# Small transfers of a two-layer block moved between issuing queues: ScalarE's to SyncE's, one store from SyncE's to GpSimd's

## The chip, the cores and the metric

The kernel runs on one core of a Trainium2 chip. The metric is the device time of one execution in microseconds (us), the median of several runs. A profile of one execution shows what each engine did: PE (TensorE matmul) and PEld (its weight load), DVE (VectorE), ACT (ScalarE), POOL (GpSimd) and SP (SyncE). SP computes nothing; it only issues transfers. ACT and POOL both compute and issue. Each engine takes its instructions in one fixed order. "ACTq", "SPq" and "POOLq" in a row are the instructions of an engine's sequencer: transfers that it issues, waits, branches.

## The reference

Two layers of a transformer-like block on 512 latent tokens and 256 context tokens, 1024 wide. Cut to what matters:

```python
def trunk_layer(x, xc, c, c_ctx, last, ...):
    mod = silu(c) @ w_mod + b_mod                  # sh1, sc1, gt1, sh2, sc2, gt2
    proj = (x * (1 + sc1) + sh1) @ w_in            # and the same for the context
    yr = rwkv_mixer(...)                           # two directions, 4 heads of 64
    ys = s5_mixer(...)
    ya = attention_mixer(...)                      # window of 128 tokens, context, sink
    mix = concat([yr, ys, ya]) @ w_out
    x = layer_norm(ALPHA * x + gt1 * mix, ln1_g, ln1_b)
    h = x * (1 + sc2) + sh2
    y = hier_moe(h, ...)                           # 32 experts, 2 for each token
    x = layer_norm(ALPHA * x + gt2 * y, ln2_g, ln2_b)
```

The recurrent part of `rwkv_mixer` is, for each token and head, `s = s * w - (s kk) b + v k`, read out by `r`, forwards and backwards. The output is `x` of the 512 latent tokens.

## The kernel before

Each layer goes through the same stages, one after the other: the input projections with the S5 mixer (`input_side`); then RWKV, with attention, the modulation and parts of the output product laid between its steps (`rwkv`, `attention`, `mod_unit`, `mixing`); then the norms and the routing (`norm`, `Route`); then the 32 experts, whose weights are streamed from memory (`experts`); then `combine`.

RWKV works on tiles of 128 tokens, six of them in the first layer.

- `front(i)` (from L367) loads a tile of the convolved projections, computes decay, keys, values and gates, and stores them in DRAM tensors from which later steps load them in another layout: `rec` (keys `kh`, the gated keys `bt`, the values) at L461, and `atd` at L462.
- `back(i)` (from L465) loads the values back in chunks of 64 tokens (`vz`, L474), transposes with TensorE, copies from PSUM with ScalarE (`ar` L483, `bz` L495, `r` L517), forms the score matrices, and stores them: `rec` at L485 and L509, `sca` at L507, `atd` at L518.
- `inverse(b)` (from L524) loads 32x32 blocks of `sca` at L540, inverts them by substitution on VectorE and GpSimd at once, and stores the inverses at L557 to L562.
- `solve(i, d)` (from L564) loads for one tile and direction a block of scores (L571), `atd` (L573), and the inverses (L576, L578), and stores its results in `rec` at L609 and L610.
- `step(n, d)` (from L616) loads a chunk of `rec` (L625) and takes the recurrence one chunk further; `finish` (L687 on) normalizes.

Up to the change, the transfers of one such step are divided between the queues of SP and ACT: at L461 the values go out by SP, the keys by ACT; at L540 the blocks of one direction by SP, of the other by ACT; in `solve` the block of scores and one inverse by SP, `atd` and the other inverse by ACT.

`mod_unit` (L114 on) computes 128 columns of the modulation: it loads 512 KB of `w_mod` by SP (L118, two buffers), has TensorE multiply them (L127), and copies the result with ScalarE (`mres`, L129). For every 512 columns of the later four parts it loads the bias row `mrow` (L122, one buffer), adds the products to it (L141), and stores it (L143), so the next load of `mrow` waits for that store.

The units of attention, modulation and mixing that are laid between RWKV's steps are counted out by the table `FILL`; `fill('front')`, `fill('back')` and so on take so many of them. Within the stage the order on each queue is not that of the text: a planner lays out each engine's instructions when the program is built, so a transfer that goes to another queue may also be given another place.

`norm(i)` (L1621 on) ends in `affine` (L1658 on): ACT scales the tile, POOL multiplies and adds a row (L1661, L1662), and SP stores the result as `x1` (L1663), which `combine` loads after the experts. SP's queue also carries the experts' weights (L1824).

The transfers of the change in the text before:

```python
for src, r, c, q in ((kh[:, d], 0, 0, nc.scalar), (bt[:, d], 64, 0, nc.scalar), (VT[i], 0, 256, nc.sync)):
    q.dma_start(rec[z, :, r:r + 64, c:c + 256], src)        # L461
nc.scalar.dma_start(vv[0:64], rec[slot[i, 0], :, 0:64, 256:512]...)   # L474
nc.sync.dma_start(x1[r], t)                                  # L1663
```

Of the kernel before, what the change touches and what calls it, by code (L numbers as in the profile page):

```python
# [61 lines left out]
def row(ap):  # L62

    return ap.rearrange("(o n) -> o n", o=1)
# [49 lines left out]
def mod_unit(k, l, mp, c0, n, bufs=2):  # L114

    nc = k.nc
    wt = mp.tile([128, 8, n], F32, name='wmod', bufs=bufs)
    nc.sync.dma_start(wt, k.a['w_mod'][l].rearrange("(p k) n -> p k n", k=8)[:, :, c0:c0 + n])  # L118
    v, f = c0 // 1024, c0 % 512
    if v >= 2 and f == 0:  # L120
        k.mrow = mp.tile([2, 512], F32, name='mrow', bufs=1)
        nc.scalar.dma_start(k.mrow, row(k.a['b_mod'][l, c0:c0 + 512]).to_broadcast([2, 512]))  # L122
    b = k.bank()
    p = b[:, 0:n]
    for kk in range(8):
        g = kk % 4
        nc.tensor.matmul(p[32 * g:32 * g + 32, :], k.cc[:, kk, :], wt[:, kk, :], start=kk < 4, stop=kk >= 4, tile_position=(0, 32 * g))  # L127
    r = mp.tile([128, n], F32, name='mres', bufs=bufs)
    nc.scalar.copy(r, p)  # L129
    p2 = b[:, n:] if n < 512 else k.bank()  # L130
    if v < 2:
        cols, bc = k.cols[l]
        j0, m = c0 // 128, n // 128
        for j in range(m):
            nc.tensor.matmul(p2[:, 2 * j:2 * j + 2], r[:, 128 * j:128 * j + 128], k.sel, start=True, stop=True)
        nc.vector.scalar_tensor_tensor(cols[:, v, j0 % 8:j0 % 8 + m, :], p2[:, 0:2 * m].rearrange("p (j s) -> p j s", s=2), float(v),
                                       bc[:, j0:j0 + m, None].to_broadcast([128, m, 2]), op0=ALU.add, op1=ALU.add)
        return
    nc.tensor.matmul(p2[0:2, 0:n], k.sel, r, start=True, stop=True)
    o = k.mrow[:, f:f + n]  # L140
    nc.vector.scalar_tensor_tensor(o, p2[0:2, 0:n], 1.0 if v == 4 else 0.0, o, op0=ALU.add, op1=ALU.add)  # L141
    if f + n == 512:
        nc.scalar.dma_start(k.dram('modrow%d' % l, [2, 4, 1024])[:, v - 2, c0 % 1024 - f:c0 % 1024 + n], k.mrow)  # L143

# [178 lines left out]
def rwkv(k, l, st, cvd, Y, ys, streams, fill):  # L325


    nc, tc = k.nc, k.tc
# [7 lines left out]
    V, G, A = nc.vector, nc.gpsimd, nc.scalar  # L336

    rec = k.dram('rec%d' % l, [12, 2, 128, 1024])
    sca = k.dram('sca%d' % l, [12, 8, 128, 64])
    atd = k.dram('atd%d' % l, [12, 128, 2, 256])  # L340
# [6 lines left out]
    GM, VT, GL = {}, {}, {}  # L347
# [3 lines left out]
    inv_o = k.dram('inv_out', [96, 64, 64])  # L351
# [15 lines left out]
    def front(i):  # L367
# [89 lines left out]
        for d in range(2):  # L457
            z = slot[i, d]

            for src, r, c, q in ((kh[:, d], 0, 0, nc.scalar), (bt[:, d], 64, 0, nc.scalar), (VT[i], 0, 256, nc.sync)):  # L460
                q.dma_start(rec[z, :, r:r + 64, c:c + 256], src)  # L461
            nc.sync.dma_start(atd[z, :, 0], at[:, d, :])  # L462
        F[i] = at, rh, bt, kh

    def back(i):  # L465

        out = emit_ctx or i >= 2
        k.stream = GS
        at, rh, bt, kh = F.pop(i)
        n = 2 if out else 1  # L470
        j = len(done) % 2
        done.append(i)
        vv = vz[j]
        nc.scalar.dma_start(vv[0:64], rec[slot[i, 0], :, 0:64, 256:512].rearrange("c t x -> t c x"))  # L474
        for d in range(2):
            z = slot[i, d]

            ar = Fp.tile([128, 2, 2, 2, 64], F32, name='ar', bufs=2)
            p = k.bank()
            for s, src in ((0, at), (1, rh))[0:n]:  # L480
                for q in range(2):
                    tr(k, p[:, 256 * s + q * 128:256 * s + q * 128 + 128], src[:, d, q * 128:q * 128 + 128])
                A.copy(ar[:, s].rearrange("p c q t -> p q c t"), p[:, 256 * s:256 * s + 256].rearrange("p (q c t) -> p q c t", q=2, c=2))  # L483
            if out:
                nc.scalar.dma_start(rec[z, :, :, 640:768].rearrange("c p x -> p c x"), ar[:, 1].rearrange("p c q t -> p c (q t)"))  # L485

            bk = bz[(2 * j + d) % 2]
            p = k.bank()
            for s, src in ((0, bt), (1, kh)):
                for q in range(2):  # L490
                    tr(k, p[:, 256 * s + q * 128:256 * s + q * 128 + 128], src[:, d, q * 128:q * 128 + 128])
                pv = p[:, 256 * s:256 * s + 256].rearrange("p (q c t) -> p q c t", q=2, c=2)
                for hp in range(2):
                    r_ = slice(64 * hp, 64 * hp + 64)
                    A.copy(bk[r_, hp, :, :, 1 - s, :], pv[r_])  # L495

            sc = Fp.tile([128, 2, 2, 2, 2, 64], F32, name='sc', bufs=2)
            for hp in range(2):
                p = k.bank()
                pv = p.rearrange("p (c q s t) -> p c q s t", c=2, q=2, s=2)  # L500
                for q in range(2):
                    for cp in range(2):
                        nc.tensor.matmul(pv[:, cp, q, 0:n, :], bk[:, hp, q, cp].rearrange("p s t -> p (s t)"),  # L503
                                         ar[:, 0:n, cp, q, :], start=True, stop=True)
                for s in range(n):
                    V.tensor_tensor(sc[:, s, :, hp], pv[:, :, :, s, :], k.msk[d][:, None, s:s + 1, :].to_broadcast([128, 2, 2, 64]), op=ALU.mult)
            nc.sync.dma_start(sca[z].rearrange("a p t -> p a t"), sc[:, 0].rearrange("p c h q t -> p (c h q) t"))  # L507
            if out:
                nc.sync.dma_start(rec[z, :, :, 768:1024].rearrange("c p x -> p c x"), sc[:, 1].rearrange("p c h q t -> p c (h q t)"))  # L509

            p = k.bank()
            for h in range(4):
                q, hp = divmod(h, 2)
                for cp in range(2):
                    nc.tensor.matmul(p[64 * cp:64 * cp + 64, 64 * h:64 * h + 64], sc[:, 0, cp, hp, q, :], vv[:, cp, 64 * h:64 * h + 64], start=True, stop=True)
            r1 = Fp.tile([128, 256], F32, name='r1', bufs=2)
            A.copy(r1, p[:, 0:256])  # L517
            nc.scalar.dma_start(atd[z, :, 1], r1)  # L518

    def dblk(ap, s0, q):  # L520

        return bass.AP(tensor=ap.tensor, offset=ap.offset + s0 * 4096 + 2080 * q, ap=[[4096, 24], [64, 32], [1, 32]])

    def inverse(b):  # L524


        R = 4
# [8 lines left out]
        for q in range(2):  # L536
            for d, t, o in ((0, Bm, 24 * q), (1, tm, 64 + 24 * q)):
                src = bass.AP(tensor=sca.tensor, offset=sca.offset + (6 * b + 3 * d) * 65536 + (64 + 32 * q) * 64 + 32 * q,
                              ap=[[8192, 24], [64, 32], [1, 32]])
                (nc.scalar if d else nc.sync).dma_start(t[o:o + 24], src)  # L540
        V.tensor_copy(Bm[64:112], tm[64:112].rearrange("p i t -> p t i"))
        for x, r0, n in ((Xl, 0, R), (Xh, R, 32 - R)):
            G.memset(x, 0.0)
# [11 lines left out]
        for q in range(2):  # L555
            f, v = slice(24 * q, 24 * q + 24), slice(64 + 24 * q, 88 + 24 * q)
            nc.sync.dma_start(dblk(inv_o, s0, q)[:, 0:R], Xl[f])  # L557
            nc.sync.dma_start(dblk(inv_o, s0, q)[:, R:32], Xh[f])
            nc.scalar.dma_start(dblk(inv_o, s0 + 24, q), tm[v])
        nc.sync.dma_start(inv_t[s0:s0 + 24], tm[0:24])  # L560
        nc.scalar.dma_start(inv_t[s0 + 24:s0 + 48, 0:R], Xl[88:112])
        nc.scalar.dma_start(inv_t[s0 + 24:s0 + 48, R:32], Xh[88:112])  # L562

    def solve(i, d):  # L564

# [4 lines left out]
        ab = Q.tile([128, 8, 32], F32, name='ab', bufs=SB)  # L570
        nc.sync.dma_start(ab[u:u + 32], sca[z, :, u:u + 32, v:v + 32].rearrange("a p t -> p a t"))  # L571
        at = Q.tile([128, 2, 256], F32, name='atl', bufs=SB)
        nc.scalar.dma_start(at, atd[z])  # L573
        x = Q.tile([128, 4, 64], F32, name='x', bufs=SB)
        for cp in range(2):
            nc.sync.dma_start(x[64 * cp:64 * cp + 64], inv_o[s0 + 4 * cp:s0 + 4 * cp + 4].rearrange("h i t -> i h t"))  # L576
        t = Q.tile([128, 8, 32], F32, name='xt', bufs=SB)
        nc.scalar.dma_start(t[u:u + 32], inv_t[s0:s0 + 8].rearrange("h i t -> i h t"))  # L578

        p = k.bank()  # L580
        w = Q.tile([128, 4, 32], F32, name='xw', bufs=2)
# [18 lines left out]
        for cp in range(2):  # L600
# [5 lines left out]
                nc.tensor.matmul(p[64:128, 256 + 64 * h:320 + 64 * h], x[own[cp], hq, :], at[own[cp], 1, 64 * h:64 * h + 64], start=True, stop=True)  # L606
            A.activation(xa[:, cp], p[:, 0:128], AF.Copy, scale=-1.0)
            V.tensor_scalar(W[64:128, cp], p[64:128, 256:512], -1.0, None, op0=ALU.mult)
        nc.scalar.dma_start(rec[z, :, :, 512:640].rearrange("c p x -> p c x"), xa)  # L609
        nc.sync.dma_start(rec[z, :, 64:128, 256:512].rearrange("c t x -> t c x"), W[64:128])  # L610

    chain = (tuple(range(12)), (3, 2, 1, 0, 11, 10, 9, 8, 7, 6, 5, 4))
# [934 lines left out]
def mixing(k, l, sO, sR, before, yd, ys, x_src, x1, hd, NTOK):  # L1547
# [73 lines left out]
    def norm(i):  # L1621
# [36 lines left out]
        def affine():  # L1658
            V.tensor_scalar(sb[:, 1:2], mv[:, 0:1], sb[:, 0:1], -1.0, op0=ALU.mult, op1=ALU.mult)
            A.activation(t, t, AF.Identity, bias=sb[:, 1:2], scale=sb[:, 0:1])  # L1660
            G.tensor_tensor(t, t, lg, op=ALU.mult)  # L1661
            G.tensor_tensor(t, t, lb, op=ALU.add)  # L1662
            nc.sync.dma_start(x1[r], t)  # L1663
        return hT, affine

    groups = [g for g in ((0, 1), (3, 4), (2, 5)) if g[0] >= t0]
# [603 lines left out]
```

## Time and profile before

| | |
|---|---|
| time before, median of 3 runs | 2894.11 us (2893.8 to 2897.02) |
| the profiled execution's own time | 2882.98 us |
| its span, first to last instruction | 2881.2 us |
| granted TensorE clock, mean of the span | 0.871 of full speed |
| PE busy | 2219.2 us (77%) |
| PEld busy | 1487.5 us (52%) |
| DVE busy | 1185.8 us (41%) |
| POOL busy | 823.0 us (29%) |
| ACT busy | 523.3 us (18%) |

The profiled execution took 2882.98 us, of which 2881.2 us are its span. Busy time leaves out what a sequencer does, so the time in which ACT issues a transfer, or waits to be allowed to, is idle time of ACT in this table. A row on a wait names the engine and line that waited and, behind the arrow, what ended the wait; "issue" stands for time in which the profile shows nothing that was waited for.

### The profile page before, as it was taken

What the parts mean: (1) busy time and instruction counts of PE and PEld (TensorE: products, weight loads), DVE (VectorE), ACT (ScalarE), POOL (GpSimd) and SP (SyncE); (2) the same over time, 40 slices, a digit from 0 to 9 for tenths busy, and PEclk for the clock granted to TensorE, in tenths of its full rate; (3) what the DMA queues carried; (4) which work ended last, traced back from release to release, by engine and by line L of the source; (5) the groups of instructions that cost most, each with busy time, mean ns of one, the idle gap of its engine ahead of it and who ended that gap; (6) DMA issues with size and microseconds to landing.
All of it is one profiled execution on the core that took longest, in us unless ns stands there. A gap on an engine that the chain in (4) does not pass through costs nothing. (4 is left out here: it accounts for less than half of the span.)

```text
span 2881.2 us, 43454 instructions
## 1 busy us (share of the span) xinstructions
PE 2219.2 (77%) x16189; PEld 1487.5 (52%) x16189; DVE 1185.8 (41%) x2830; ACT 523.3 (18%) x1264; POOL 823.0 (29%) x1131
## 2 busy tenths in 40 slices
PE   5898677789874978989955787677898488788882
PEld 4786445567432544555525675455555254454441
DVE  7872554665556100000016873456645711111113
ACT  3222233223001100001015222233110100000001
POOL 2651322431544011101016652333324510111002
PEclk8999788789986999999987898579699699999996
DMA  8334466665627899989974324446784589998995
GB/s 241 93 94 116 141 179 185 175 189 163 220 93 265 351 418 371 391 329 379 388 279 121 83 56 142 117 128 161 212 244 140 230 355 418 416 379 331 384 419 201
DMA packets 404797, 691.34 MB, mean 240 GB/s; under 512 B 134755, under 2 KB 310627, under 8 KB 388097
## 3 DMA queue, kind: packets, MB, share of 16 engines
q1 hardware_dynamic: 311808, 600.10, 58.1%
q10 hardware_dynamic: 78880, 64.32, 7.5%
q0 software_dynamic: 13792, 22.61, 2.1%
q8 instruction: 211, 3.46, 0.5%
q14 instruction: 106, 0.86, 0.1%
HBM read 607.98 MB, written 95.44 MB: 244 GB/s over the span
## 5 line engine op out<-in xcount | busy, mean ns | idle before, releaser
L1762 PE MATMUL b_m<-w,xT 128*64 128x256 f32 x4928 | 593.7, 396 | 128.8 <-DMA w<-in_expert_w_gate_dram 80.2
L1762 PEld LDWEIGHTS b_m<-w,xT 128*64 128x64 f32 x4928 | 391.9, 142 | 333.3 <-issue 148.0
L243 PE MATMUL b_m<-xT,win 128*128 128x256 f32 (+1 forms) x1416 | 275.8, 355 | 7.0 <-POOL xT L167 3.5
L243 PEld LDWEIGHTS b_m<-xT,win 128*128 128x128 f32 x1416 | 232.8, 202 | 41.0 <-POOL xT L167 4.4
L1786 PE MATMUL b_m<-w,aT 128*64 128x512 f32 x1024 | 231.0, 592 | 1.1 <-issue 0.6
L1775 DVE COPY aT<-b_m 128x256 f32<-128x256 f32 x64 | 27.2, 425 | 474.4 <-PE b_m L59 474.4
L1792 POOL DMA_INDIRECT yb<-y,dx x64 | 63.9, 998 | 419.7 <-DVEq L1907 245.2
L1786 PEld LDWEIGHTS b_m<-w,aT 128*64 128x64 f32 x1024 | 76.2, 137 | 117.3 <-issue 108.3
L1764 ACT ACTIVATE act<-b_m 128x256 f32<-128x256 f32 x64 | 24.6, 384 | 566.8 <-PE b_m L1762 566.8
L1765 DVE TENSOR_TENSOR act<-act,b_m 128x256 f32<-128x256 f32 x64 | 27.0, 422 | 233.5 <-PE b_m L1762 233.5
L877 PE MATMUL b_a<-kz,qb 128*128 128x128 f32 (+2 forms) x416 | 111.9, 415 | 8.2 <-ACT pr L898 6.1
L1582 PE MATMUL b_a<-wo,yt 128*128 128x512 f32 x240 | 112.4, 618 | 0.0
L1792 POOL DMA_INDIRECT yb<-yo,dx x13 | 12.9, 994 | 291.7 <-ACTq L1907 166.2
L127 PE MATMUL b_a<-wmod,cc 128*32 128x128 f32 x1280 | 64.2, 315 | 40.0 <-DMA wmod<-in_w_mod_dram 28.0
L877 PEld LDWEIGHTS b_a<-kz,qb 128*128 128x128 f32 x416 | 78.2, 237 | 32.2 <-issue 13.0
L59 PE MATMUL b_a<-idf,pr 128*128 128x128 f32 x320 | 58.4, 304 | 34.3 <-DVE pt L921 11.5
L503 PE MATMUL b_g<-ar,bz 128*128 128x128 f32 (+1 forms) x384 | 66.2, 337 | 11.7 <-ACT bz L495 11.6
L1855 POOL DMA_INDIRECT xg<-hd,ix x32 | 33.0, 1031 | 146.8 <-PE b_m L59 105.2
L503 PEld LDWEIGHTS b_g<-ar,bz 128*128 128x128 f32 x384 | 61.8, 248 | 22.3 <-ACT bz L495 18.0
L1582 PEld LDWEIGHTS b_a<-wo,yt 128*128 128x128 f32 x240 | 45.2, 196 | 51.2 <-issue 50.3
L127 PEld LDWEIGHTS b_a<-wmod,cc 128*32 128x32 f32 x1280 | 37.7, 122 | 58.0 <-DMA wmod<-in_w_mod_dram 29.9
L551 POOL TENSOR_TENSOR tl<-Bm,Xh 112x4 f32<-112x4 f32 (+13 forms) x112 | 38.0, 339 | 95.0 <-DVE Xh L552 53.7
(539 smaller groups left out, 3979.9 us busy)
## 6 DMA issues: line engine op xcount, KB each, us to landing
w<-in_expert_w_gate_dram SPq DMA_DIRECT2D x64, 2048.0 KB
w<-in_expert_w_up_dram SPq DMA_DIRECT2D x64, 2048.0 KB
w<-in_expert_w_down_dram SPq DMA_DIRECT2D x64, 2048.0 KB
wmod<-in_w_mod_dram SPq DMA_DIRECT2D x80, 512.0 KB
rec<-rec SPq DMA_DIRECT2D x40, 512.0 KB
win<-in_w_in_dram SPq DMA_DIRECT2D x16, 1024.0 KB
wmod<-in_w_mod_dram SPq DMA_DIRECT2D x4, 2048.0 KB
sca<-sc SPq DMA_DIRECT2D x24, 256.0 KB
```

The lines of the kernel that those rows point to most:

```text
L59: k.nc.tensor.transpose(out, x, k.idf[r:r + n, r:r + n])
L127: nc.tensor.matmul(p[32 * g:32 * g + 32, :], k.cc[:, kk, :], wt[:, kk, :], start=kk < 4, stop=kk >= 4, tile_position=(0, 32 * g))
L243: nc.tensor.matmul(p[:, :n], wt[u][:, kk, j * 128:j * 128 + 128], xT[v][:, kk, c0:c0 + n], start=kk == 0 and q == 0, stop=kk == 7 and q == 2)
L503: nc.tensor.matmul(pv[:, cp, q, 0:n, :], bk[:, hp, q, cp].rearrange("p s t -> p (s t)"), ar[:, 0:n, cp, q, :], start=True, stop=True)
L551: eng.tensor_tensor(t[:, 0:n, j:32], Bm[:, r0:r1, j:j + 1].to_broadcast([112, n, w]), x.to_broadcast([112, n, w]), op=ALU.mult)
L877: nc.tensor.matmul(dst, qb[:, 2 * v + e, :], kz[:, v, r, 128 * keys[c][0]:128 * keys[f - 1][0] + 128], start=c == 0 or (c == 4 and r == 0) ...
L1582: nc.tensor.matmul(ps[h], y[:, kt, :], wo[:, kt, 512 * h:512 * h + 512], start=kt == 0, stop=kt == 5)
L1762: mm = nc.tensor.matmul(p[64 * h:64 * h + 64, 0:256], xT[:, kk, :], w[:, kk, 256 * h:256 * h + 256], start=kk == 0, stop=kk == 7)
L1775: k.nc.vector.tensor_copy(aT, pa[:, 0:256].rearrange("p (j x) -> p j x", j=2))
L1786: nc.tensor.matmul(py[64 * s:64 * s + 64, :], aT[:, j, 64 * h:64 * h + 64], wd[:, q, 512 * s:512 * s + 512], start=q == 0, stop=q == 3)
L1792: sc = nc.gpsimd.indirect_dma_start(out=yb, out_offset=bass.IndirectOffsetOnAxis(ap=dst, axis=0), in_=y, in_offset=None, bounds_check=3071 ...
L1855: return nc.gpsimd.indirect_dma_start(out=out, out_offset=None, in_=hd, in_offset=bass.IndirectOffsetOnAxis(ap=idx, axis=0), bounds_check= ...
```

## The change

All of RWKV's transfers that ACT issued go to SP's queue, as do the load and the store of `mrow`; the store of `x1` goes from SP's queue to POOL's. Nothing else is touched: no shape, no buffer, no arithmetic. The numbers of what moves: 24 each of the stores of `kh`, `bt` (L461), `r1` (L518) and `xa` (L609), 20 of `ar` (L485), 12 loads of `vz` (L474), 24 each of the loads at L573 and L578, 8 loads at L540, 8, 4 and 4 stores at L559, L561 and L562, 16 loads and 16 stores of `mrow`: 232 transfers from ACT to SP, and 10 stores of `x1` from SP to POOL.

```diff
@@ mod_unit
-        nc.scalar.dma_start(k.mrow, row(k.a['b_mod'][l, c0:c0 + 512]).to_broadcast([2, 512]))
+        nc.sync.dma_start(k.mrow, row(k.a['b_mod'][l, c0:c0 + 512]).to_broadcast([2, 512]))
...
-        nc.scalar.dma_start(k.dram('modrow%d' % l, [2, 4, 1024])[:, v - 2, c0 % 1024 - f:c0 % 1024 + n], k.mrow)
+        nc.sync.dma_start(k.dram('modrow%d' % l, [2, 4, 1024])[:, v - 2, c0 % 1024 - f:c0 % 1024 + n], k.mrow)
@@ rwkv, front
-            for src, r, c, q in ((kh[:, d], 0, 0, nc.scalar), (bt[:, d], 64, 0, nc.scalar), (VT[i], 0, 256, nc.sync)):
-                q.dma_start(rec[z, :, r:r + 64, c:c + 256], src)
+            for src, r, c in ((kh[:, d], 0, 0), (bt[:, d], 64, 0), (VT[i], 0, 256)):
+                nc.sync.dma_start(rec[z, :, r:r + 64, c:c + 256], src)
@@ rwkv, back
-        nc.scalar.dma_start(vv[0:64], rec[slot[i, 0], :, 0:64, 256:512].rearrange("c t x -> t c x"))
+        nc.sync.dma_start(vv[0:64], rec[slot[i, 0], :, 0:64, 256:512].rearrange("c t x -> t c x"))
...
-                nc.scalar.dma_start(rec[z, :, :, 640:768].rearrange("c p x -> p c x"), ar[:, 1].rearrange("p c q t -> p c (q t)"))
+                nc.sync.dma_start(rec[z, :, :, 640:768].rearrange("c p x -> p c x"), ar[:, 1].rearrange("p c q t -> p c (q t)"))
...
-            nc.scalar.dma_start(atd[z, :, 1], r1)
+            nc.sync.dma_start(atd[z, :, 1], r1)
@@ rwkv, inverse
-                (nc.scalar if d else nc.sync).dma_start(t[o:o + 24], src)
+                nc.sync.dma_start(t[o:o + 24], src)
...
-            nc.scalar.dma_start(dblk(inv_o, s0 + 24, q), tm[v])
+            nc.sync.dma_start(dblk(inv_o, s0 + 24, q), tm[v])
...
-        nc.scalar.dma_start(inv_t[s0 + 24:s0 + 48, 0:R], Xl[88:112])
-        nc.scalar.dma_start(inv_t[s0 + 24:s0 + 48, R:32], Xh[88:112])
+        nc.sync.dma_start(inv_t[s0 + 24:s0 + 48, 0:R], Xl[88:112])
+        nc.sync.dma_start(inv_t[s0 + 24:s0 + 48, R:32], Xh[88:112])
@@ rwkv, solve
-        nc.scalar.dma_start(at, atd[z])
+        nc.sync.dma_start(at, atd[z])
...
-        nc.scalar.dma_start(t[u:u + 32], inv_t[s0:s0 + 8].rearrange("h i t -> i h t"))
+        nc.sync.dma_start(t[u:u + 32], inv_t[s0:s0 + 8].rearrange("h i t -> i h t"))
...
-        nc.scalar.dma_start(rec[z, :, :, 512:640].rearrange("c p x -> p c x"), xa)
+        nc.sync.dma_start(rec[z, :, :, 512:640].rearrange("c p x -> p c x"), xa)
@@ mixing, norm, affine
-            nc.sync.dma_start(x1[r], t)
+            G.dma_start(x1[r], t)
```

## Rows read from the trace of the kernel before

**Rows 1.** Stretches: us, PE PEld DVE ACT POOL busy (instructions), clock, DMA share, GB/s.

```profile
295.00:520.00 225.00, 152.72 (x1286) 106.06 (x1287) 114.94 (x299) 72.38 (x223) 72.17 (x133) 0.80 0.62 175
520.00:730.00 210.00, 180.24 (x1911) 136.09 (x1910) 117.48 (x326) 57.10 (x196) 55.55 (x139) 0.84 0.65 177
1800.00:2010.00 210.00, 152.55 (x1096) 114.02 (x1098) 121.58 (x290) 73.58 (x222) 74.45 (x146) 0.75 0.50 136
2010.00:2200.00 190.00, 168.49 (x1724) 108.55 (x1721) 95.24 (x243) 33.44 (x115) 57.21 (x102) 0.86 0.76 215
```

**Rows 2.** Waits of PE, 295 to 520 us: total us, times, longest us.

```profile
PE b_a L127 <- DMA wmod<-in_w_mod_dram: 15.5, 5, 6.0
PE b_a L127 <- ACT pr L898: 10.0, 3, 5.6
...
PE b_g L59 <- ACT r L517: 0.2, 1, 0.2
```

**Rows 3.** Waits of PE, 1800 to 2010 us.

```profile
PE b_g L59 <- ACT bz L495: 8.0, 3, 4.7
...
PE b_a L934 <- ACT pr L898: 0.3, 1, 0.3
```

**Rows 4.** Timeline of ACT, 290 to 372 us: start, duration, what [idle before <-releaser].

```profile
294.79 5.61 ACTq L461 DMA_DIRECT2D rec<-av  x1
300.44 0.63 ACT L344 ACTIVATE av<-av 128x512 f32<-128x512 f32 x1 [10.85 <-issue]
...
353.91 4.59 ACTq L461 DMA_DIRECT2D rec<-av  x1
...
363.03 0.27 ACTq L143 DMA_DIRECT2D modrow<-mrow  x1
...
369.36 0.27 ACTq L122 DMA_DIRECT2D mrow<-in_b_mod_dram  x1
```

**Rows 5.** Timeline of PE, 290 to 372 us.

```profile
301.59 2.08 PE L416 MATMUL b_f<-sg,cum 128*128 128x256 f32 x4 [7.03 <-ACT rk L397]
...
359.26 1.08 PE L127 MATMUL b_a<-wmod,cc 128*32 128x128 f32 x16 [5.65 <-ACT pr L898]
```

**Rows 6.** Issues of one line each: ns min/median/max, first and last start us.

```profile
L461 SPq DMA_DIRECT2D rec<-vt x24: 489/542/1862, 280.0 to 1920.5; - x24
L461 ACTq DMA_DIRECT2D rec<-kd x24: 500/556/3128, 292.6 to 1930.8; - x24
L461 ACTq DMA_DIRECT2D rec<-av x24: 500/530/5605, 293.3 to 1934.0; - x24
...
L2058 POOL DMA_DIRECT2D kvd<-qs x8: 542/550/804, 259.6 to 1765.4; - x8
```

**Rows 7.** Waits of SP's queue, 295 to 520 us.

```profile
SPq L509 <- DMA rec<-av: 12.3, 2, 10.0
...
SPq L118 <- PE b_a L127: 10.3, 9, 2.5
```

**Rows 8.** Waits over the whole span.

```profile
PE b_a L127 <- DMA wmod<-in_w_mod_dram: 28.0, 11, 6.0
```

**Rows 9.** Waits of SP's queue over the whole span.

```profile
SPq L1663 <- POOL q L1662: 59.3, 5, 14.2
SPq L1663 <- DVE q L1641: 51.8, 4, 24.3
```

**Rows 10.** Timeline of SP's queue, 850 to 875 us.

```profile
855.70 14.83 SPq L1663 DMA_DIRECT2D x<-q  x2
871.70 0.33 SPq L1824 DMA_DIRECT2D w<-in_expert_w_gate_dram  x1
```

**Rows 11.** Timeline of POOL, 850 to 875 us.

```profile
870.13 0.73 POOL L708 TENSOR_TENSOR y<-y,b_gn_b 128x256 f32<-128x256 f32 x1
870.94 0.72 POOL L711 TENSOR_TENSOR y<-y,sq 128x256 f32<-128x256 f32 x1
```

**Rows 12.** The costliest groups of the page: busy us, mean ns of one, idle before.

```profile
L1855 POOL DMA_INDIRECT xg<-hd,ix x32 | 33.0, 1031 | 146.8 <-PE b_m L59 105.2 <-issue 21.9 <-DVE r_li L1536 12.4
```

## The prediction

> **What bounds the kernel now.** I read the stretches first, then who PE waits for in the stretches that the change touches, then what ACT's queue did in those waits, and last SP's queue, which takes the work over. The page's chain of the work that ended last reaches back only over the last 20 us, so it says nothing of these stages, and I go by PE's waits.
>
> RWKV's stage has two parts in each layer [rows 1]: `front`, `back` and the first inversion (225 and 210 us), and `solve` and the steps (210 and 190 us). In the second parts PE is busy for 180.2 of 210 and 168.5 of 190 us: PE sets the end there. In the first parts it is busy for only 152.7 of 225 and 152.6 of 210 us, at a granted clock of 0.80 and 0.75 of the higher of its two levels (2.4 GHz). That is where this change can pay.
>
> PE's waits in the first parts are mostly on ACT: ten rows, from the 10.0 us on `pr` to the 0.2 us on `r`, add up to 44.8 us in the first layer [rows 2], and twelve, from 8.0 to 0.3 us, to 40.7 us in the second [rows 3]. Yet ACT is busy for only 72.4 and 73.6 us of these parts [rows 1]. What holds it are its transfers. The store of `bt` at 294.79 us keeps ACT's queue for 5.61 us, and the next ACTIVATE, 10.85 us after ACT's last, starts right behind it [rows 4]; PE stood still for 7.03 us up to 301.59 us and was released by the copy after that ACTIVATE [rows 5]. At 353.91 us the same line takes 4.59 us [rows 4], inside a wait of PE of 5.65 us [rows 5]. The median issue on this line is 0.53 us, the longest 5.605 [rows 6], so it is the long ones that hurt.
>
> **The change part by part.** *ACT is freed.* 232 transfers leave ACT's queue, with their waits. Of PE's 85.5 us of waits on ACT in the first parts, the two examples show 5.61 + 4.59 = 10.2 of 12.7 us, 0.8, spent under a long issue. Many smaller waits hold no long issue, so I take 0.6 of all: 51 us. Bounds: 10.2 us, if the two examples are all, and 85.5 us. When a wait falls away, PE goes on to the next thing that is late. VectorE is next: it is busy for half of these parts (114.9 of 225, 121.6 of 210 [rows 1]) and feeds most of what ACT feeds. I let 70% come through: -36 us. In the second parts I take nothing: PE is close to full and its waits on ACT are short; between a few us of loss and a few of gain.
>
> *SP takes them.* At the 0.53 and 0.556 us of line 461 [rows 6], the nearest rows, the 232 make some 125 us of issue over the 835 us of the four parts, beside what SP has. The issuing itself is hidden, as SP computes nothing; what can hurt is order, as SP stands still at the first transfer that is not ready. For most of the moved ones that order is there already: values, scores, `W` and one inverse of the same tile go by SP now, and the consumer waits for both halves. SP also waits for ACT today: 12.3 us before L509 until ACT's store of `bt` had landed [rows 7]; on one queue that store is issued before. New are the transfers that must first wait for another to land: 12 loads of `vz` (for the values' store) and 16 of `mrow` (for its store). The store of `mrow` goes out at 363.03 us and the next load at 369.36 [rows 4], 6.3 us in which, on SP, no `w_mod` would be fetched. The modulation's loads are what PE waits for from SP: 28.0 us, 11 times, 2.5 us each [rows 8]. I allow for three more such waits, +8 us. Bounds: -10 us, if SP loses its waits for ACT, and +56 us, if there are 22 more.
>
> *x1 from POOL.* SP stood before this store for 59.3 us until POOL's addition and for 51.8 us until a VectorE operation on its tile [rows 9]. What that held back was not late for it: the second of the two stores at 855.70 us leaves SP at 870.53, and the first experts' weights behind it go out at 871.70 [rows 10], when POOL's addition for `y` ends (870.94 + 0.72 us) [rows 11], whose memory they take over. So freeing SP is worth nothing there, as POOL covers it; without that cover it would be the 1.1 us between the two. POOL now issues ten stores. Its other stores cost it 0.550 us, its gathers 1.031 us [rows 6, 12]; I take 1 us, as the store is larger than the first kind. Six of the ten have nothing pressing behind them; behind the store at 870 us stand the normalization of `y` [rows 11], then the output product and the routing. With four such places that is up to 4 us, of which POOL's own pauses take half: +2 us. Bounds: -1 and +10 us.
>
> Sum: -36 + 8 + 2 = -26 us. Against the profiled execution's 2882.98 us that is 2857; it ran 11.1 us under the median of the runs shown, 2894.11, so the forecast for the median is **2868 us**.
>
> A rule of the Trainium skill speaks against this: "DMA: Bandwidth & Descriptors", section "Issuing engines are not separate DMA queues", holds that another issuing engine saves only the sequencer's time to start a transfer, usually small beside the transfer. By it the sum would be 0. The trace differs on "small": the issue took up to 5.605 us [rows 6], on an engine that computes.
>
> **The rivals.** *A, no change (0.12).* ACT's lateness is only where the wait shows; behind it PE would wait as long for VectorE, and the 36 us go into other waits: some 2892 us. For: DVE is busy for half of the stage. Against: ACT starts work at once after a long store [rows 4], so its inputs were there. It is what the skill's rule above would give.
>
> *B, SP becomes the line (0.18), slower.* Place: L122 and L474 on SP, with the `w_mod` loads behind them. Price: 2.5 us for each further load that is late [rows 8]. The gain of 36 us is used up at 14 more; with 22 more, 33 of the 80 units that lie in these stages, it is 56 - 36 + 2 = +22 us: 2916 us. For: SP already stands for 10.3 us in the first part at `w_mod`'s buffer, 9 times [rows 7], and everything moved would stand behind it. Against: the moved transfers' siblings stand there today.
>
> The Trainium skill has a mechanism for B: "DMA: Bandwidth & Descriptors", "Queues, rings and completion order", says that SP and ACT each have rings of their own on the same 16 engines, which take turns between them. By it the small transfers, on SP's rings, would lose their turn beside the 512 KB loads. No row here shows the landing of these transfers.
>
> *C, more than forecast (0.15).* All 51 us come through, and with fewer pauses the clock of the first parts moves toward that of the second (0.75 to 0.86, 0.80 to 0.84 [rows 1]). A third of what that would save on PE's busy time (152.6 x 0.11/0.86 + 152.7 x 0.04/0.84 = 27 us) is 9: 2894 - 60 = 2834 us.
>
> *D, it does not do what it says (0.06).* Each queue's order is laid out anew when the program is built, and a worse one could cost as much as ACT's freedom gives: 2894, either way by 20.
>
> **How the numbers follow.** The forecast with its surroundings, -10 to -45 us, has 0.49. 0.2% is 5.8 us, about what a measurement of this kernel can tell from no change. Faster: the forecast, C and the better half of D, 0.67. The same: A, and a hundredth of the borders of the others, 0.13. Slower: B and the rest of D, 0.20. The range takes in C to 2830 and most of B to 2912; outside lie B's upper half and the full bounds, under 0.2. Within the forecast alone it would be 2849 to 2884.
>
> **What would show it.** Right: in the stretch from 295 us PE's waits on `pr`, `mres`, `rk` and `bz` shrink to a third, no long issue is left among ACT's rows there, and the first part ends some 15 us earlier in each layer, at the same PE busy time or a little less. SP's rows on L461 show the long issues in place of ACT's, with no reader waiting. For x1, POOL shows ten transfers of about 1 us, and the weights start when they did. Wrong: PE's wait on `wmod` grows past 60 us, or PE's waits on VectorE take over what ACT's lost; and if a stage that the change does not touch (the experts) moves by more than the forecast, the cause is not here.

## The result, and the profile after

The changed kernel takes 2999.82 us (median of 4 runs, 2996.21 to 3003.79) against 2893.95 us before: a ratio of 1.0368, 95% interval 1.0347 to 1.0389, some 106 us **slower**. The forecast was 2868 us, and the range ended at 2912. The profiled execution took 2997.61 us, its span 2995.2.

The loss lies in RWKV's stage. Below are the stretches of each layer from the first load of `front` (L373) to the first norm of the mixing (L1647), first of the kernel before, then of the kernel after; the columns are those of [rows 1].

```profile
255.00:756.00 501.00, 389.08 (x3479) 278.63 (x3477) 259.57 (x671) 140.08 (x442) 155.72 (x306) 0.83 0.62 176
...
1753.00:2234.00 481.00, 373.79 (x3110) 260.24 (x3108) 260.13 (x609) 120.05 (x369) 171.33 (x298) 0.80 0.58 164
```

```profile
255.00:841.00 586.00, 393.80 (x3542) 282.72 (x3540) 286.80 (x700) 141.01 (x441) 165.29 (x313) 0.79 0.54 153
...
1833.00:2347.00 514.00, 362.44 (x3109) 251.06 (x3107) 258.12 (x607) 119.81 (x368) 169.84 (x298) 0.79 0.54 154
```

The stage grew by 85 and 33 us, while PE's busy time moved by 5 and -11 us: PE waits more. (The first stretch of after also holds 63 matmuls more, and the stretch behind it is 11 us shorter. The profiled execution before ran 11 us under its median, so beside its profile the others look some 10 us slower than by the medians.) For whom PE waits in the first part of the first layer, 290 to 560 us of the kernel after, to be set beside [rows 2]:

```profile
PE b_a L127 <- DMA wmod<-in_w_mod_dram: 45.1, 8, 15.5
PE b_g L515 <- DVE sm L892: 13.2, 1, 13.2
PE b_a L877 <- DVE qb L831: 11.6, 1, 11.6
PE b_g L515 <- DVE sc L506: 7.3, 2, 4.5
PE b_g L515 <- DMA vz<-rec: 6.7, 1, 6.7
PE b_a L139 <- ACT mres L129: 4.8, 10, 1.1
PE b_g L59 <- ACT r L517: 3.6, 2, 2.3
PE b_g L59 <- ACT bz L495: 3.3, 6, 1.0
...
PE b_g L503 <- ACT bz L495: 2.3, 5, 0.5
```

The waits on ACT have shrunk: these four rows are 14.0 us and all rows on ACT of this stretch 15.4, where they were 44.8. As the first part now ends later, the whole stretches of the stage are the fairer measure: there the waits on ACT fell from 50.0 to 27.5 us in the first layer and from 55.2 to 31.0 in the second. In their place stand loads and, in the first layer, VectorE. Over the whole span, PE's waits on the loads of RWKV and of the modulation, with `wmod` at 66.1 us where it was 28.0 [rows 8]:

```profile
PE b_a L127 <- DMA wmod<-in_w_mod_dram: 66.1, 18, 15.5
...
PE b_f L585 <- DMA xt<-inv_t: 35.5, 2, 23.1
PE b_g L515 <- DMA vz<-rec: 33.8, 3, 19.5
```

Before, `xt` made 0.5 us of waits there, and `vz` has no row.

The longest wait for `wmod` ends at 360.32 us. The timeline of SP's queue in the kernel after, and behind it the row of PE:

```profile
340.35 3.14 SPq L462 DMA_DIRECT2D atd<-e  x1
343.54 0.49 SPq L461 DMA_DIRECT2D rec<-kd  x1
344.08 2.80 SPq L461 DMA_DIRECT2D rec<-av  x1
346.92 3.21 SPq L461 DMA_DIRECT2D rec<-vt  x1
350.17 2.60 SPq L462 DMA_DIRECT2D atd<-e  x1
352.87 2.93 SPq L118 DMA_DIRECT2D wmod<-in_w_mod_dram  x2
```

```profile
360.32 1.08 PE L127 MATMUL b_a<-wmod,cc 128*32 128x128 f32 x16 [15.47 <-DMA wmod<-in_w_mod_dram]
```

Two loads of `wmod` leave only at 352.87 us, behind 12.5 us of stores that keep the queue nearly without a gap; PE had read both buffers by 339.1 us. The long issues that ACT had [rows 4] are SP's now.

### The profile page after: what moved, and what is told of

The parts are those of the page before. It is cut to its first block, busy times and chain, and to the rows that moved or that the text cites. A ratio compares the mean times of both kernels' runs of the same rounds, so it can differ in the third digit from the quotient of the medians.

```text
span 2995.2 us, 43446 instructions
## 1 busy us (share of the span) xinstructions
PE 2208.4 (74%) x16189; PEld 1479.1 (49%) x16189; DVE 1199.0 (40%) x2830; ACT 525.2 (18%) x1264; POOL 830.9 (28%) x1141
## 5 line engine op out<-in xcount | busy, mean ns | idle before, releaser
L877 PE MATMUL b_a<-kz,qb 128*128 128x128 f32 (+2 forms) x416 | 102.9, 388 | 23.9 <-DVE qb L831 22.8
L127 PE MATMUL b_a<-wmod,cc 128*32 128x128 f32 x1280 | 67.8, 333 | 69.6 <-DMA wmod<-in_w_mod_dram 66.1
L877 PEld LDWEIGHTS b_a<-kz,qb 128*128 128x128 f32 x416 | 71.4, 220 | 43.7 <-DVE qb L831 23.1
L515 PE MATMUL b_g<-vz,sc 128*64 128x64 f32 x384 | 24.7, 261 | 57.6 <-DMA vz<-rec 33.8
L884 DVE TENSOR_REDUCE mx<-b_a 128x1 f32<-128x512 f32 (+1 forms) x80 | 48.4, 629 | 43.0 <-PE b_a L883 22.8
L893 POOL TENSOR_TENSOR sm<-sink,sm 128x2 f32<-128x2 f32 x40 | 8.6, 214 | 202.9 <-DVE sm L891 202.6
```

The source lines that it names most:

```text
L877: nc.tensor.matmul(dst, qb[:, 2 * v + e, :], kz[:, v, r, 128 * keys[c][0]:128 * keys[f - 1][0] + 128], start=c == 0 or (c == 4 and r == 0) ...
L884: V.tensor_reduce(mx[:, 0, r:r + 1], aa[r][:, 0:w], axis=AX.X, op=ALU.max)
```

## The experiments

From this my theory was the **queue**: SP issues its transfers one after the other, so loads that PE needs stand behind stores. The rival was the **order**: the planner lays out every engine's instructions when the program is built, and it laid them out anew.

### One part at a time

Each of four kernels makes one part of the change and leaves the rest as before:

```diff
-            nc.sync.dma_start(x1[r], t)
+            G.dma_start(x1[r], t)
```

That is the first. The others take from the change's diff only the lines of the modulation (L122, L143), of front and back (L461 for `kh` and `bt`, L474, L485, L518), and of the inversion and the solve (L540, L559, L561, L562, L573, L578, L609).

> Only x1's store moved, to Pool's queue. Queue theory (SP's one queue in order, loads that PE needs next behind stores that are not ready) puts the loss in RWKV's stage: here -3 to +10 us. Rival (x1's stores on Pool's queue hold up Pool's additions for the rows behind): +30 us or more. Rival (the planner's new order of the engines' instructions): little, as this part hardly changes the order, -5 to +5 us.

> Only the modulation's two small transfers moved, from ACT's queue to SP's. Queue theory: the next load of mrow waits on SP until the store before it has landed, with the modulation's weights behind it; PE's wait on wmod in RWKV's first part of layer 0 grows from 28.0 us over the whole kernel to 40 or more, and the time by +5 to +30 us. Rival (only the transfers of RWKV itself matter): PE's wait on wmod as before, time -10 to +5 us.

> Only the transfers of front and back moved to SP: the stores of kh and bt, the load of vz, the stores of ar and of r1. Queue theory: PE's waits on ACT in the first parts fall (44.8 us to under 20 in layer 0), its waits on DMA (vz, wmod) rise by as much or more; the time by -10 to +40 us. Rival (ACT's relief is the whole of this part and the loss is in the inversion and the solve): -20 to -40 us.

> Only the transfers of the inversion and of solve moved to SP: the loads of tm, atl and xt, the stores of the inverses and of xa. Queue theory: xt's load stands behind SP's waits for the inverses and for xa; PE's waits on xt appear (two of over 10 us in the kernel with all parts), the second parts get 15 to 30 us longer each, the time +25 to +70 us. Rival (this part costs little alone, and only the sum of all the moved transfers overfills SP): -5 to +15 us, and the four parts together well under the 106 us of the whole.

| moved | median, us | before, us | ratio, 95% interval |
|---|---|---|---|
| x1 alone | 2900.04 | 2897.37 | 1.0003, 0.9982 to 1.0024 |
| modulation | 2924.06 | 2897.37 | 1.0098, 1.0069 to 1.0127 |
| front and back | 2911.31 | 2897.37 | 1.0057, 1.0035 to 1.0079 |
| inversion and solve | 2977.76 | 2897.37 | 1.0296, 1.0253 to 1.0338 |

x1 costs nothing. The other three cost 27, 14 and 80 us, more than the whole together. By their times the first three lie inside what the queue theory expected, the last 10 us above it. By their waits not all do: with the modulation's transfers moved, PE's wait on `wmod` over the whole kernel is 21.0 us, less than the 28.0 before [rows 8], where 40 were expected, and yet the time is 27 us longer. Each kernel is also planned anew, so these runs don't tell the two theories apart.

### Order and queue apart

The planner may be told that one instruction of an engine has to be issued behind another. Such an edge between each instruction of an engine and the next one pins its order. The kernels below carry at the end of the program, for both RWKV stages and for all five engines, the order that the planner gave to another kernel. In short form:

```python
traced = list(tc.nc.cur_bb.bb.instructions)
last = {}
for n in ORDER:
    i = traced[n]
    if i.engine in last:
        tc.add_manual_dep(i, last[i.engine].name, issue_order_only)
    last[i.engine] = i
```

A transfer that goes by another queue takes there the place that it had in the overall order. So queue and order can be changed one without the other.

> All the change's transfers on their new queues, but every engine's instructions pinned to the order that the planner gave them in the kernel before; on SP the moved transfers stand where they stood in that overall order. Queue theory (SP in order, needed loads behind stores that are not ready): about as slow as the change, +70 to +110 us, with PE's waits on xt, vz and wmod as there. Order theory (the planner's new order of the engines does it, and the queue itself would pay): -35 to +10 us.

> No transfer moved, but every engine's instructions pinned to the order that the planner gave them in the changed kernel. Queue theory: -10 to +25 us, as ACT's own transfers keep their queue. Order theory: +70 to +110 us, with the last loads of front's tiles in the first layer as late as in the changed kernel.

| us against the kernel before | transfers as before | transfers moved |
|---|---|---|
| order of the kernel before | 0 | +10.7 (ratio 1.0036, 1.0018 to 1.0055) |
| order of the changed kernel | +123.4 (1.0426, 1.0384 to 1.0467) | +106 (1.0368, 1.0347 to 1.0389) |

**My theory falls as the main cause.** With every transfer moved but the old order, some 11 us are lost, just over the order theory's range; with no transfer moved but the new order, 123, even more than it had expected. In the new order the moved transfers don't add to the loss: with them it is 17 us less, by intervals that just touch. The kernel before with its own order pinned was not run; the nearest is the run with inversion and solve below (0.9986), which leaves little room for a cost of the pin itself. The traces bear the pin out: in the first stretch of the run with all transfers moved, all 671 instructions of VectorE come in the order of the kernel before. The same stretches, first of the run with the queues moved, then of the run with the new order:

```profile
255.00:771.00 516.00, 390.17 (x3465) 278.49 (x3464) 261.60 (x671) 140.19 (x441) 155.97 (x305) 0.81 0.61 170
1771.00:2259.00 488.00, 368.50 (x3108) 257.50 (x3106) 258.02 (x608) 120.33 (x368) 170.20 (x298) 0.81 0.57 161
```

```profile
255.00:842.00 587.00, 407.70 (x3539) 293.43 (x3537) 285.54 (x699) 140.95 (x441) 164.46 (x313) 0.78 0.54 152
1829.00:2363.00 534.00, 380.88 (x3109) 264.35 (x3107) 256.52 (x607) 120.60 (x368) 169.50 (x298) 0.77 0.52 148
```

The waits of PE in the run with the new order, 255 to 600 us and then 2060 to 2446 us:

```profile
PE b_a L139 <- ACT mres L129: 18.4, 13, 10.5
PE b_f L585 <- DMA xt<-inv_t: 14.5, 1, 14.5
PE b_g L515 <- DMA vz<-rec: 14.2, 3, 9.6
PE b_a L127 <- DMA wmod<-in_w_mod_dram: 13.7, 6, 4.6
PE b_a L877 <- DVE qb L831: 11.6, 1, 11.6
```

```profile
...
PE b_f L585 <- DMA xt<-inv_t: 18.0, 1, 18.0
```

The holes at `xt`, `vz` and `qb` are those of the changed kernel (its `qb` too is 11.6 us, once), with ACT issuing its own transfers, for which PE waits at `mres`. Only `wmod` is as short as before (29.9 us over the whole span, 28.0 before): that one is the queue's. What the new order looks like shows in the last three loads of `front`'s tiles in the first layer, on SP's timeline, before and after:

```profile
293.31 0.66 SPq L373 DMA_DIRECT2D cvt<-cvd  x1
308.41 0.98 SPq L373 DMA_DIRECT2D cvt<-cvd  x1
350.06 0.42 SPq L373 DMA_DIRECT2D cvt<-cvd  x1
```

```profile
376.17 0.65 SPq L373 DMA_DIRECT2D cvt<-cvd  x1
422.25 0.65 SPq L373 DMA_DIRECT2D cvt<-cvd  x1
462.01 1.66 SPq L373 DMA_DIRECT2D cvt<-cvd  x1
```

The last three tiles begin 83 to 114 us later, and in the run with the new order alone at 373.95, 419.91 and 457.53 us. What follows them is late as well: PE comes to the solve (L585) while the inverses are still on their way. But these loads only show that the order is another one; they don't measure its cost. With front and back alone moved and the planner free they are as late (377.15, 395.97 and 457.06 us), and 14 us are lost; with inversion and solve alone they start as early as before (the last at 347.56), and 80 us are lost.

The costly parts were run with the old order too:

> The transfers of front and back alone on SP, with the order of the kernel before pinned (without the pin this part took +14 us). Order theory: the relief of ACT shows in both layers, -20 to -40 us. Queue theory: 0 to +25 us, as vz and wmod stand behind stores whatever the order.

> The transfers of the inversion and the solve alone on SP, with the order of the kernel before pinned (without the pin this part took +80 us). Queue theory: +50 to +90 us. Order theory: -5 to +15 us.

Front and back: 0.9994 (0.9969 to 1.0019); inversion and solve: 0.9986 (0.9963 to 1.0009), where it cost 80 us with the planner free. So both losses were the order's. But front and back gave no gain either, and PE's waits say why. First layer, 255 to 530 us, with all transfers moved and the order pinned:

```profile
PE b_a L127 <- DMA wmod<-in_w_mod_dram: 52.7, 11, 10.8
...
PE b_f L388 <- ACT e L442: 6.1, 1, 6.1
```

and in the second, 1771 to 2020 us of the same run:

```profile
PE b_g L515 <- DVE sc L506: 27.3, 7, 11.1
PE b_a L59 <- DVE pr L906: 21.3, 3, 12.7
```

The waits on ACT are down to 11.8 and 10.6 us by all rows, and `wmod` took their place in the first layer (15.5 us before [rows 2]; 53.7 with only front and back moved), VectorE in the second. But VectorE is not the last cause there. It waits for Pool (18 us at the softmax sums of L903, where it was 5), and Pool waits for attention's loads `kr` and `qr` (L844, L857), which SP now issues between the stores of L461. Pool's waits in the second layer, before (1753 to 2013 us) and in this run (1771 to 2020 us):

```profile
POOL kr L828 <- DMA kr<-kvd: 7.8, 1, 7.8
POOL qr L828 <- DMA qr<-qd: 6.4, 2, 4.5
```

```profile
POOL kr L828 <- DMA kr<-kvd: 22.5, 2, 12.7
POOL qr L828 <- DMA qr<-qd: 16.5, 2, 14.7
```

So in both layers loads on SP's queue took the place of ACT. That is the queue theory at its true size: it eats the gain and, with every transfer moved, some 11 us more.

### Which engine's order

> All the change's transfers on their new queues and PE's instructions alone pinned to the order of the kernel before; the planner is free with the other engines, as in the changed kernel. If it is PE's order that costs (solves and scores put before what they need): 0 to +30 us. If the order on VectorE, ScalarE and Pool costs as much: +50 to +110 us.

> All the change's transfers on their new queues; PE, VectorE, ScalarE and Pool pinned to the order of the kernel before, SP's order left to the planner. If the order of the computing engines is what costs: 0 to +25 us, near the run with everything pinned (+11). If it is the place that the planner gives the transfers on SP: +50 to +110 us.

> All the change's transfers on their new queues; SP alone pinned to the order of the kernel before, the computing engines left to the planner. If the order of the computing engines is what costs: +60 to +110 us. If it is the transfers' place on SP: +0 to +30 us.

In these the loop above skips engines; for the first, with the other two alike for SP:

```diff
     i = traced[n]
+    if i.engine != mybir.EngineType.PE:
+        continue
```

PE alone in the old order: 1.0323 (1.0285 to 1.0362); PE keeps its order and the others come late, once by 29.3 us at L382. All but SP: 1.0350 (1.0300 to 1.0400). SP alone: 1.0204 (1.0153 to 1.0256). So **neither half suffices**. In the second of them every computing engine has the order of the kernel before, and only the place of transfers on SP differs from the run that lost 11 us; it loses 103. Its waits of PE, 255 to 560 us:

```profile
PE b_a L127 <- DMA wmod<-in_w_mod_dram: 49.8, 9, 12.6
PE b_f L382 <- ACT gc L424: 16.8, 1, 16.8
PE b_g L515 <- DVE sc L506: 15.5, 2, 11.4
PE b_f L388 <- ACT e L442: 14.5, 1, 14.5
```

`wmod` is no later than with everything pinned. What is new are waits on `front`'s and `back`'s own work: that work was late. With SP alone in the old order, the computing engines' new one costs 69 us by the medians (2964.46 against 2895.56), while `wmod` stays at 29.7 us over the whole span with every transfer moved: the wait depends also on when PE asks for it. The free engines were planned against the pinned ones here, so neither run holds the changed kernel's own order, and the two losses don't add up to its 106 us. Which places in the order cost most stays open.

### Versions that beat both

If the relief of ACT is real and SP's charge eats it, another queue should keep it. The long issues were those of `kh` and `bt` [rows 4, 6]; they go to Pool's queue:

```diff
-            for src, r, c, q in ((kh[:, d], 0, 0, nc.scalar), (bt[:, d], 64, 0, nc.scalar), (VT[i], 0, 256, nc.sync)):
+            for src, r, c, q in ((kh[:, d], 0, 0, nc.gpsimd), (bt[:, d], 64, 0, nc.gpsimd), (VT[i], 0, 256, nc.sync)):
```

> The order of the kernel before pinned; only the stores of kh and bt moved, to Pool's queue, so ACT is relieved of its long issues and SP is not charged. If in the pinned runs SP's charge (PE's wait on wmod 15.5 to 53 us in the first layer) cancelled ACT's relief: -15 to -35 us, with PE's wait on wmod back under 20 us. If the relief is worth nothing because VectorE is as late: -5 to +5 us. If Pool's 48 issues hold up its own work: +5 to +20 us.

> Only the stores of kh and bt on Pool's queue, with the planner free (pinned to the order of the kernel before this gave 2849.5 us). If a new order costs whatever the transfer that causes it: +10 to +60 us on the kernel before. If only transfers on SP lead the planner astray: -30 to -50 us, as pinned.

> The order of the kernel before pinned; the stores of kh, bt, ar and r1 on Pool's queue, so ACT is relieved of 92 issues and SP is not charged. If what ACT still waits at those stores is left in PE's way: 5 to 20 us under the run with kh and bt alone (2849.5 us). If PE's rest of waits on ACT is gone with kh and bt: within 5 us of it. If Pool becomes late: 10 to 30 us over it.

With the old order pinned: 2849.52 us against 2898.87, ratio **0.9823 (0.9786 to 0.9860)**, beyond the 35 us that I had allowed. With the planner free: 0.9926 (0.9900 to 0.9951), between what either theory had expected; a new order costs here too, though no transfer went to SP. With `ar` and `r1` on Pool as well: 0.9850 (0.9802 to 0.9897), not to be told from `kh` and `bt` alone. The stretches of the pinned run with `kh` and `bt`, PE's waits in its first layer (255 to 530 us), and the issues of L461 (ns min/median/max):

```profile
255.00:748.00 493.00, 396.10 (x3473) 283.87 (x3471) 261.54 (x671) 140.51 (x442) 175.77 (x329) 0.82 0.65 178
1746.00:2199.00 453.00, 361.70 (x3109) 248.90 (x3107) 257.71 (x607) 120.01 (x368) 192.11 (x322) 0.83 0.62 174
```

```profile
PE b_a L127 <- DMA wmod<-in_w_mod_dram: 28.4, 9, 6.0
PE b_f L388 <- ACT e L442: 8.4, 1, 8.4
```

```profile
L461 POOL DMA_DIRECT2D rec<-kd x24: 796/798/1044, 291.6 to 1898.9; - x24
L461 POOL DMA_DIRECT2D rec<-av x24: 796/807/938, 292.7 to 1899.7; - x24
```

The stage is 8 and 28 us shorter, and PE's waits on ACT over these stretches are 22.3 and 31.8 us (50.0 and 55.2 before). PE waits 28.4 us for `wmod`, half of what it does with SP charged, though not under the 20 I had expected. Pool's 48 issues are busy time of some 0.8 us each and never long.

The second layer of the run with front and back on SP had been 461 us long instead of 481, so that was tried by itself. The queue in the code is `(nc.sync if l else nc.scalar)`, with the planner free; a second kernel has its order pinned and no transfer moved.

> Front's and back's transfers on SP in the second layer only; the planner leaves the order of the first layer as before and gives the second the order that it had when the part was moved in both. There the stretch from the first load to the norm took 461 us instead of 481. If that gain belongs to the stage and not to the one execution: -15 to -25 us, a version that beats both kernels. Otherwise -5 to +8 us.

> The same order of every engine as in the run with the second layer's front and back on SP, pinned, but no transfer moved. Order theory (the order is what counts): as that run within 8 us. Relief theory (the gain there is ACT's freedom): 0 to +15 us against the kernel before.

0.9927 (0.9905 to 0.9949), 21 us faster; the order alone: 0.9965 (0.9944 to 0.9986), 12 us faster. So a new order may also come out better: by the medians about half of this gain was the order and half the transfers, though the two intervals touch. The same move that loses 14 us in both layers gains 21 in one.

## Why the prediction was wrong, step by step

- **The step that failed is the order: the sum has no term for it, and rival D put it too small.** Under "SP takes them" I reasoned that for most of the moved transfers "that order is there already". In D I wrote that a worse order "could cost as much as ACT's freedom gives", 20 us either way, with a chance of 0.06, and had no row for its size. The new order costs 123 us with nothing else changed, and between the pinned and the free run of the full change 95 (106 less 11). Its sign was open, as the second layer alone shows.
- **ACT is freed: right, and if anything too small.** PE's waits on ACT fell from 44.8 us to 15.4 in the first part. The run with only `kh` and `bt` moved, to Pool, gained 49 us by the medians; I had -36, and rival C 51 before its clock term. (C's 2834 us leaves out the +8 and +2 of the other two parts.)
- **SP takes them, +8 us: mis-sized.** In the old order PE's wait on `wmod` grew by 37 us in the first layer (52.7 less 15.5), and in the second attention's loads came late. The first was inside my bound of 56, and the mechanism was rival B's. The argument against B, that "the moved transfers' siblings stand there today", didn't hold: a sibling's place says nothing of the time that SP spends on one more issue. The 125 us of issue that I called hidden are in the trains that `wmod` stands behind. With 37 for the 8, the sum is +3 us by my -36 and -10 by the 49 of Pool's run; +10.7 was measured, and how the rest divides, the second layer's loads among it, no run shows.
- **Second parts at nothing: wrong with the order, right without it.** There PE waits up to 23.1 us for `xt` in the changed kernel; pinned, the part that I took at nothing measures 0.9986.
- **x1 from POOL, +2 us: right within its bounds.** The ratio is 1.0003, and its issues on Pool take less than the 1 us I allowed:

```profile
L1663 POOL DMA_DIRECT2D x<-q x10: 553/646/678, 848.7 to 2391.8; - x10
```

- **Rival A** looked right of the second layer with the order pinned: there the waits on ACT turned into waits on VectorE. But behind VectorE stood SP's loads, and with Pool as the queue that layer gained 28 us, so VectorE's lateness was no fixed limit.
- Of the tests, "PE's wait on `wmod` grows past 60 us" came true (66.1), but it pointed at the smaller cause.

By the Trainium skill, "DMA: Bandwidth & Descriptors", section "Issuing engines are not separate DMA queues", the engine that issues matters only by the sequencer's time, usually small beside the transfer. Here the median issue is small (0.53 us), but the long ones are not, and the 48 stores that went from ACT to Pool gave 1.8%: in this kernel PE waited for results of ACT that stood behind such issues.

The Trainium skill, "DMA: Bandwidth & Descriptors", section "Queues, rings and completion order", says that each DMA engine takes turns between the queue rows and goes through each ring in order; by it loads of `wmod` that share SP's rings with the moved stores could land later. The traces don't bear that out: where PE waited for `wmod`, it started 4.4 to 10.7 us after the load's issue before, and 4.2 to 9.7 us after it with every transfer moved in the old order. The loads were issued late; they didn't land later.

## What to carry to other kernels

Where a planner lays out the program, a moved transfer is two changes, and the second is a throw of the dice: pin the old order and run the move in it, and run the new order without the move, before anything is said of queues. Here the better queue for the stores was the one with the fewest urgent loads behind them, and that was not the engine that computes nothing. And an issue counts as hidden only if nothing that a reader waits for stands behind it in that queue.

## What the runs showed of the hardware

The same stores of `kh` and `bt` hold their queue very differently: on ACT up to 5.605 us with a median of 0.53 [rows 6], on SP in the pinned run with front and back up to 3.595, on Pool never over 1.044. What a long issue waits for on ACT and SP, the rows don't say:

```profile
L461 SPq DMA_DIRECT2D rec<-kd x24: 478/514/2619, 292.3 to 1939.8; - x24
L461 SPq DMA_DIRECT2D rec<-av x24: 483/512/3595, 293.5 to 1940.4; - x24
```

The granted clock is lower where the holes are longer: of the higher level (2.4 GHz) it is 0.83 and 0.80 in the two stretches before, and 0.78 and 0.77 with the new order alone, where PE stood longer between its groups. PE's busy time is 19 and 7 us longer there, the first with 60 matmuls more.
